# A two-layer hybrid trunk on one core: retention's gates computed as a block problem of seven products, with the mixer's work in another order

## The chip, the cores and the metric

The kernel runs on one core of one Trainium2 chip. The metric is the device time of one execution in microseconds (us). PE is the matrix engine, PEld its loading of the stationary operand, DVE the vector engine, ACT the scalar engine, POOL the GpSimd engine; SP issues most of the transfers, POOL the transfers that add to what already lies in the target ("accumulating").

## The reference, cut to what matters

Two layers; the input is one sequence of 512 rows of 1024 values, all float32. A layer's mixer projects the rows with one matrix of 9216 columns, runs three branches (retention, chunked attention, differential attention), weighs each with a gate, and projects the sum; a SwiGLU block follows.

```python
h = jnp.einsum('bsd,de->bse', x, w_in[l])
rq, rk, rv, rg, cq, ck, cv, dq, dk, dv, gates = jnp.split(h, splits, axis=-1)
o_a = _retention(rq, rk, rv, rg, ret_norm_g[l])      # rq and rk turned by a rotary table
o_b = _chunk_attention(cq, ck, cv, ca_rel_bias[l])
o_c = _diff_attention(dq, dk, dv, lam, lambda_init, da_norm_g[l])
g = jax.nn.sigmoid(gates + b_merge[l]).reshape(B, S, N_BRANCHES, D)
merged = (g[:, :, 0] * (o_a @ w_branch_a[l]) + g[:, :, 1] * (o_b @ w_branch_b[l])
          + g[:, :, 2] * (o_c @ w_branch_c[l]))
x = _layer_norm(DEEPNORM_ALPHA * x + merged @ w_out[l], ...)
ffn = (silu(u_gate) * u_up) @ w_ffn_out[l]           # u = x @ w_ffn_in[l]
x = _layer_norm(DEEPNORM_ALPHA * x + ffn, ...)
```

The change touches the 1024 columns of `gates` that belong to retention (`g[:, :, 0]`), one tile of the third branch's gates, and the order in which rq, rk, rv, rg, cv, dv and these gates are made.

## The kernel before, in words

**Numbers.** Each float32 operand is carried as a high part and the remainder. A product is therefore three matmuls (`mm3`, L126 to L128: high by high, low by high, high by low), all at the same shapes. A piece of a weight arrives by DMA in a staging tile `st` (four buffers of 1 MB), ACT copies its rounded high part to `wh` (L158 or L396), and DVE subtracts to get the low part `wl` (L159 or L403). `wh` and `wl` have three buffers each (`AHEAD`), so the copy of a block waits until PE has ended the block three places before it; a staging buffer is free again when DVE has read it for the last time.

**Block problems.** The large projections take two column groups and two halves of the 1024 inputs as a 2x2 block matrix and compute the result with seven products instead of eight. `u_two` (L911) lists the seven by name: m1, m2, y, v, x, g, h. A product's weight side is a staged block or a sum of blocks: the sum `a` is loaded by SP and a second block is added to it by an accumulating DMA from POOL (`more`, L192); the sum `d` is a loaded block to which DVE adds (L271); `c` is loaded and accumulated like `a`, and `e` is a further sum. Classes `Close`, `Early`, `Late` and `Known` differ in when blocks are loaded and added. The activation side is a quarter of x, or a left or right sum of quarters, which `s_q(k)` makes on DVE and ACT (L425 to L436, with the split of L110 and L116). A product is 24 matmuls of 512 columns and each of its lines is `pf<-...`; afterwards ACT copies the bank (`tc<-pf`, L928), or DVE adds it or subtracts it (L933, L938, L943). Where a text writes w, p and q, these are the problems of cv with dv and of the two halves of rv with rg.

**Gates.** The gates of a branch are made by `u_gate(br, i)`, 256 columns at a time: 48 matmuls of 512 columns with x as the stationary operand (`proj_T`, `pt<-xTh,wh`) and a tanh on ACT (L1283) whose tile goes to DRAM. Retention's four such items stand between the products of the mixer.

**Order.** `start` and the list behind it (L1467 to L1500) are the items of the mixer in the order in which PE runs them. The lists beside an item are functions that are called after its two halves. Weights are fetched `AHEAD` items early. A scheduler then emits one program for each engine, and each engine takes its own instructions strictly in that order. The indices COPIED_AT and ADDED_AT say at which item copies and sums for the later SwiGLU part are made.

**Opening.** In layer 0 PE first makes rq and rk tile by tile as weights land, with two weight tiles of 256 columns, then two gate tiles with a third (`u_first`, L913). Each rq or rk bank goes through the rotary table at once: `rotary` (L505) copies the swapped halves on ACT (L510) and multiplies and adds on DVE (L512 to L514).

## Time and profile before

| | us |
|---|---|
| median of 3 runs | 1844.89 (1843.74, 1844.89, 1845.23) |
| the profiled execution, its own time | 1843.16 |
| its span, first to last instruction | 1841.3 |
| PE busy in the span | 1830.8 |
| DVE busy | 1375.4 |
| ACT busy | 1035.2 |

The mean granted clock of PE was 0.999. A row of the timeline gives the start, the duration, the engine, the line and the tiles; a bracket at its end is the idle time before it with what ended it. A row of a group gives count, busy time and the mean of one in ns. PE's matmuls overlap, so what one costs is the distance from one start to the next, not its own duration.

### The profile page before, as it was taken

The page shows a single profiled execution, that of the slowest core. Times are in us where ns is not written, and L with a number is a line of the kernel's source. Part 1 is how long each engine was busy: PE and PEld are TensorE (multiplying, and loading weights), DVE is VectorE, ACT ScalarE, POOL GpSimd, SP SyncE. Part 2 cuts the span into 40 slices and gives each one's busy share as a digit, 9 for nine tenths or more (in the row PEclk, how much of TensorE's full clock was granted, in tenths as well). Part 3 has the DMA queues.
Part 4 walks back from the last instruction along what each step waited for, and adds up shares of the span by engine and source line. Part 5 has one row for each costly group of instructions (what it writes and reads, how often), then busy time and mean ns, then how long its engine had stood idle before and what let it go on. Part 6 is the DMA issues. An engine that isn't in the chain of part 4 may idle for free.

```text
span 1841.3 us, 23376 instructions
## 1 busy us (share of the span) xinstructions
PE 1830.8 (99%) x8718; PEld 1530.6 (83%) x8718; DVE 1375.4 (75%) x2077; ACT 1035.2 (56%) x1651; POOL 156.3 (8%) x170
## 2 busy tenths in 40 slices
PE   9999999999999999999999999999999999999998
PEld 8888888888887888888888888888888878888886
DVE  6866766767669786789787767566775797867887
ACT  5555555576545645555555556556766465455552
POOL 2001000001001000001020010000010010000010
PEclk9999999999999999999999999999999999999999
DMA  9689755566475876687685887555565677667783
GB/s 286 185 272 240 194 159 171 140 185 165 117 226 148 201 221 162 160 257 195 218 252 175 245 217 208 181 150 154 165 160 137 195 180 183 208 177 180 225 219 113
DMA packets 248065, 351.12 MB, mean 191 GB/s; under 512 B 9605, under 2 KB 112113, under 8 KB 247953
## 3 DMA queue, kind: packets, MB, share of 16 engines
q1 hardware_dynamic: 213088, 281.84, 46.2%
q0 software_dynamic: 34720, 67.55, 21.3%
q8 instruction: 68, 1.11, 0.2%
q14 instruction: 45, 0.36, 0.1%
q10 hardware_dynamic: 144, 0.26, 0.0%
HBM read 327.54 MB, written 64.01 MB: 213 GB/s over the span
## 4 chain that ended last, share of the span: by engine, by line
PE 97%; DVE 2%; ACT 1%; DMA 1%; issue 0%; POOL 0%; DVEq 0%; POOLq 0%; ACTq 0%
PE pf L126 16%; PE pf L128 15%; PE pf L127 15%; PE pt L126 14%; PE pt L128 13%; PE pt L127 13%; PE ptr L587 1%; PE psc L548 1%; PE pco L1159 1%; PE psc L547 1%; PE ph L1540 1%; PE pdo L1236 1%; DVE wl L403 1%; DMA st<-out10c 1%; ACT wh L396 0%; PE pro L128 0%
## 5 line engine op out<-in xcount | busy, mean ns | idle before, releaser
L403 DVE TENSOR_TENSOR wl<-st,wh 128x2048 fp32r<-128x2048 f32 (+2 forms) x173 | 377.9, 2185 | 153.3 <-ACT wh L396 152.8
L396 ACT CAST wh<-st 128x2048 fp32r<-128x2048 f32 (+1 forms) x168 | 315.2, 1878 | 237.9 <-PE pf L128 110.8
L126 PE MATMUL pt<-xTh,wh 128*128 128x512 f32 x832 | 326.8, 393 | 0.0
L128 PE MATMUL pt<-xTh,wl 128*128 128x512 f32 x832 | 324.4, 390 | 0.0
L127 PE MATMUL pt<-xTl,wh 128*128 128x512 f32 x832 | 324.2, 390 | 0.0
L159 DVE TENSOR_TENSOR wl<-st,wh 128x1024 fp32r<-128x1024 f32 (+2 forms) x158 | 166.6, 1073 | 60.8 <-ACT wh L158 47.5
L158 ACT CAST wh<-st 128x1024 fp32r<-128x1024 f32 (+2 forms) x158 | 143.6, 929 | 83.4 <-PE pt L127 58.1
L128 PEld LDWEIGHTS pt<-xTh,wl 128*128 128x128 f32 x832 | 156.2, 188 | 33.1
L127 PEld LDWEIGHTS pt<-xTl,wh 128*128 128x128 f32 x832 | 156.4, 188 | 31.2 <-DVE xTl L757 0.3
L126 PEld LDWEIGHTS pt<-xTh,wh 128*128 128x128 f32 x832 | 156.4, 188 | 31.0
L126 PE MATMUL pf<-wh,xTh 128*128 128x512 f32 x384 | 151.1, 395 | 0.2
L128 PE MATMUL pf<-wh,xTl 128*128 128x512 f32 x384 | 149.2, 390 | 0.0
L127 PE MATMUL pf<-wl,xTh 128*128 128x512 f32 x384 | 149.2, 389 | 0.0
L126 PE MATMUL pf<-wh,s12h 128*128 128x512 f32 x296 | 116.7, 394 | 0.0
L126 PE MATMUL pf<-wh,s43h 128*128 128x512 f32 x296 | 116.0, 392 | 0.0
L127 PE MATMUL pf<-wl,s12h 128*128 128x512 f32 x296 | 115.4, 390 | 0.0
L127 PE MATMUL pf<-wl,s43h 128*128 128x512 f32 x296 | 115.3, 389 | 0.0
L128 PE MATMUL pf<-wh,s43l 128*128 128x512 f32 x296 | 114.9, 389 | 0.0
L128 PE MATMUL pf<-wh,s12l 128*128 128x512 f32 x296 | 114.7, 390 | 0.0
L928 ACT COPY tc<-pf 128x512 f32<-128x512 f32 x96 | 55.2, 588 | 72.0 <-PE pf L128 71.0
L126 PEld LDWEIGHTS pf<-wh,xTh 128*128 128x128 f32 x384 | 72.1, 188 | 17.1 <-ACT xTh L110 1.5
L128 PEld LDWEIGHTS pf<-wh,xTl 128*128 128x128 f32 x384 | 72.1, 188 | 16.0 <-DVE xTl L116 0.7
(384 smaller groups left out, 3685.9 us busy)
## 6 DMA issues: line engine op xcount, KB each, us to landing
st<-in_w_in SPq DMA_DIRECT2D x53, 1024.0 KB, 6.7
st<-in_w_ffn_in SPq DMA_DIRECT2D x46, 1024.0 KB, 5.3
st<-in_w_in SPq DMA_DIRECT2D x48, 512.0 KB, 5.0
st<-in_w_ffn_in POOLq DMA_DIRECT2D x20, 1024.0 KB, 11.1
st<-in_w_in POOLq DMA_DIRECT2D x12, 1024.0 KB, 11.5
st<-in_w_ffn_out SPq DMA_DIRECT2D x12, 1024.0 KB, 5.2
th<-th SPq DMA_DIRECT2D x40, 256.0 KB, 4.8
st<-in_w_out SPq DMA_DIRECT2D x10, 1024.0 KB, 6.0
```

The lines of the kernel that those rows point to most:

```text
L126: nc.tensor.matmul(ps, lh, rh, start=start, stop=False, skip_group_check=onto)
L127: nc.tensor.matmul(ps, lh, rl, start=False, stop=False, skip_group_check=onto)
L128: nc.tensor.matmul(ps, ll, rh, start=False, stop=stop, skip_group_check=onto)
L158: return [nc.scalar.copy(self.hi[:, a:b], self.st[:, a:b]), nc.vector.tensor_sub(self.lo[:, a:b], self.st[:, a:b], f(self.hi[:, a:b]))]
L159: nc.vector.tensor_sub(self.lo[:, a:b], self.st[:, a:b], f(self.hi[:, a:b]))]
L396: nc.scalar.copy(self.hi, st)
L403: nc.vector.tensor_sub(self.lo[:, k], self.st[:, k], f(self.hi[:, k]))
L547: yield nc.tensor.matmul(ps[:, :w], self.q[j][:, n], self.k[j][:, :w], start=True, stop=False)
L548: yield nc.tensor.matmul(ps[:, :w], self.q[j][:, n], self.kl[j][:, :w], start=False, stop=True)
L587: nc.tensor.transpose(ps[:, o + P * (nt - mt):o + P * (nt - mt) + P], E[pk][:, c + P * mt:c + P * mt + P], ident)
L928: nc.scalar.copy(t[to, j], ps)
L1159: pin(nc.tensor.matmul(*ops[k], start=k == order[0], stop=k == order[-1]))
```

## The change

Retention's gates leave `u_gate` and become a fourth block problem, t, of class `Early`, over the 1024 gate columns. It uses `product_T` in place of `product`: a block of 128 by 128 of the weight is the stationary operand and a quarter of the rows, 256 columns wide, is the moving one, so a product is 48 matmuls of 256 columns. The tanh is taken on 256 columns at a time with the bias of a column tile, and a tile goes to DRAM as one half of a pair.

The order of the mixer's first part is written anew, with t's products between those of w and p, and q's behind p's. Counted over both layers, 384 `pt` matmuls of 512 columns leave (832 to 704 in each of the three lines of `mm3`), and 672 `pf` matmuls of 256 columns come in. DVE gets 17 instructions more (12 `tc` additions, 4 sums of staging tiles, and the sizes of some subtractions change), ACT 34 more, SP three transfers more and POOL four more accumulating transfers.

Three smaller things go with it: the first problem is of a new class `Grown`, whose first block grows into the sum `a`; in the opening the rq and rk banks are only copied (`raw`) and swapped on ACT, and `s_rot` does the DVE part later, behind products of t and w; values that went to DRAM come back in halves (`v_back`), and lam is computed later (`late_lam`).

```diff
-EARLY = [(0, 0), (0, 1), (0, 2), (0, 3), (2, 0)]
+EARLY = [(2, 0)]
...
+    class Grown(Early):
+        def m1(self):
+            if "made" in self.__dict__:
+                return self.__dict__.pop("made")
+            if "first" not in self.__dict__:
+                self.early()
+            self.a = self.__dict__.pop("first")
+            b = self.block(self.a)
+            self.more(self.a, 0, 1)
+            return b
...
+    def product_T(acts, name, j, wt, ps=None):
+        onto = ps is not None
+        ps = ps if onto else bank("pf")
+        for q in range(2):
+            c, o = P * (2 * j + q), 256 * q
+            for k in range(wt.nk):
+                hi, lo = acts[k].use[name]
+                mm3(ps[:, o:o + 256], wt.hi[:, k, c:c + P], wt.lo[:, k, c:c + P], hi, lo,
+                    k == q == 0 and not onto, q == 1 and k == wt.nk - 1, True)
+        return ps
...
+        def rqk_raw(i, h, ps):
+            t = g(name="raw")
+            nc.scalar.copy(t, ps)
+            raws[i, h] = t, swapped(ps, 64)
+
+        def s_rot(i, h):
+            return lambda: rqk_done((rq, rk)[i], h, *raws.pop((i, h)))
...
+                    vectors()
                     quarters(0)
+                    opening[0].made = opening[0].m1()
+                    for k in range(2):
+                        s_q(k)()
                 for i, w in enumerate(wts):
...
                         if i < 2:
-                            rqk_done((rq, rk)[i], j, ps)
+                            rqk_raw(i, j, ps)
                         else:
-                            gate_done(0, j, ps)
+                            gate_done(2, 4 * j, ps)
...
+        def gates_left(base):
+            def done(t, c):
+                i, j = divmod(t, 2)
+                m = base // 2 + j
...
+                s = g(name="th") if i and base == 0 else c
+                for q in range(2):
+                    sl = slice(256 * q, 256 * q + 256)
+                    d = 2 * m + q
+                    nc.scalar.activation(s[:, sl], c[:, sl], AF.Tanh, scale=0.5, bias=v["hb"][:, d:d + 1])
+                nc.sync.dma_start(th["pair", m][:, :, 256 * i:256 * i + 256], s.rearrange("p (q c) -> p q c", q=2))
+            return done
...
-        opening[l] = (Early if l else Close)(W, 0, 4, (CV, DV))
+        opening[l] = Grown(W, 0, 4, (CV, DV))
...
+        t = u_two(Early(W, 0, 4, (GATE, GATE + 512)), xq, gates_left(0), gates_left(4), product_T)
+        natural = []
         if l == 0:
-            start = [(u_first(),), (u_gate(0, 1), [s_q(0), s_q(1)], [s_q(2), w["a"]]), (u_gate(0, 2), [s_q(3)], [w["c"]]),
-                     (w["m1"],), (w["y"],), (w["v"],), (w["m2"], [lam])]
+            start = [(u_first(), [], [s_q(2)], [], [s_q(3)]),
+                     (w["m1"],), (w["m2"],)]
...
-            (w["x"], [p["a"]]), (u_gate(0, 3), [s_kt(0)], [s_kt(1)]), (w["g"],), (w["h"], [p["c"]]),
-            (p["m1"], [s_dh(0)]), (p["y"], [], [s_r1(0)]), (p["v"], [s_dh(1)]), (p["m2"], [], [s_r1(1)]),
-            (p["x"], [q["a"]]), (u_rqk(rq, RQ, 1), [s_kv(0)], [s_kv(1)]), (p["g"], [q["c"]]), (p["h"],),
...
+            (t["m1"], [w["c"]], natural[1:2]), (w["y"], natural[2:3]), (w["v"], [t["a"]]), (w["x"], natural[3:]), (t["m2"], [s_rot(1, 0)]),
+            (w["g"],), (t["y"], [s_kt(0)]), (w["h"], [t["c"]], [s_rot(1, 1)]), (t["v"], [p["a"]], [s_rot(0, 0)]),
+            (t["x"], [], [s_rot(0, 1)]), (p["m1"], [s_dh(0)], [s_kt(1)]), (t["g"], [late_lam]),
+            (p["y"], [], [s_r1(0)]), (t["h"], [p["c"], s_dh(1)]), (p["v"],), (p["m2"], [q["a"]], [s_r1(1)]), (p["x"],),
+            (q["m1"], [s_kv(0)], [s_kv(1)]), (p["g"],), (q["y"],), (p["h"], [q["c"]]),
```

The scheduled programs of the changed kernel show three places. The first is DVE in the opening of layer 0, where the low parts of the first blocks of w are made between quarter sums (`sa`, `sb` and their low parts `s12l`, `s43l`). Before, with the end of the third quarter's sums, the fourth quarter's, and among them the low part for w's v, the third of its blocks (`wl_634`):

```order
L435 TENSOR_TENSOR sb_542<-xf_134,sa_535 128x256
L436 TENSOR_TENSOR sb_542<-xf_122 128x256
L116 TENSOR_TENSOR s43l_546<-sb_542,s43h_545 128x512
L425 TENSOR_TENSOR sa_585<-xf_125,xf_137 128x256
L426 TENSOR_TENSOR sa_585<-sa_585,xf_125 128x256
L403 TENSOR_TENSOR wl_634<-st_631,wh_633 128x2048
L116 TENSOR_TENSOR s12l_589<-sa_585,s12h_588 128x512
L435 TENSOR_TENSOR sb_592<-xf_137,sa_585 128x256
L436 TENSOR_TENSOR sb_592<-xf_125 128x256
L271 TENSOR_TENSOR st_631<-st_631,st_549 128x2048
```

Now, with `wl_466` the low part for w's m2, in two halves:

```order
L116 TENSOR_TENSOR s43l_378<-sb_374,s43h_377 128x512
L542 TENSOR_TENSOR sw_383<-sw_383,sinr_198 128x512
L438 TENSOR_TENSOR sa_391<-xf_125,xf_137 128x256
L439 TENSOR_TENSOR sa_391<-sa_391,xf_125 128x256
L416 TENSOR_TENSOR wl_466<-st_463,wh_465 128x1024
L116 TENSOR_TENSOR s12l_395<-sa_391,s12h_394 128x512
L448 TENSOR_TENSOR sb_398<-xf_137,sa_391 128x256
L449 TENSOR_TENSOR sb_398<-xf_125 128x256
L416 TENSOR_TENSOR wl_466<-st_463,wh_465 128x1024
```

The last quarter sums stood around the third block of w; now they stand ahead of and between the halves of its second one, with the rotary's multiplications (`sw`) among them. On ACT the same place reads now as follows; `raw` and `sw` are the copies of the rq and rk banks, `wh_324` and `wh_465` the high parts for m1 and m2:

```order
L110 CAST s43h_353<-sb_350 128x512
L886 COPY raw_357<-pt_201 128x512
L409 CAST wh_324<-st_322 128x2048
L838 COPY colv_312<-pcol_310 128x64
L534 COPY sw_359<-pt_201 64x512 x2
L886 COPY raw_362<-pt_202 128x512
L534 COPY sw_364<-pt_202 64x512 x2
L409 CAST wh_465<-st_463 128x2048
L110 CAST s12h_370<-sa_367 128x512
L110 CAST s43h_377<-sb_374 128x512
L886 COPY raw_381<-pt_203 128x512
L534 COPY sw_383<-pt_203 64x512 x2
```

Behind the high part of m2 come two quarter sums' splits and the third bank's copies, on which the DVE rows above wait. The second place is DVE between t's y and t's x in layer 0 (`wl_748` and `wl_939`; `wl_820` is for w's h, `wl_872` for t's v):

```order
L416 TENSOR_TENSOR wl_748<-st_680,wh_747 128x2048
L116 TENSOR_TENSOR vhl_737<-tc12_695,vhl_737 128x2x128
L116 TENSOR_TENSOR vhl_742<-tc12_695,vhl_742 128x2x128
L980 TENSOR_TENSOR tc11_590<-tc11_590,pf_751 128x512
L541 TENSOR_TENSOR rot_781<-raw_381,cosr_197 128x512
L980 TENSOR_TENSOR tc11_620<-tc11_620,pf_789 128x512
L543 TENSOR_TENSOR rot_781<-rot_781,sw_383 128x512
L416 TENSOR_TENSOR wl_820<-st_626,wh_819 128x2048
L116 TENSOR_TENSOR rqkl_786<-rot_781,rqkh_785 128x512
```

These rows run on without a gap into the next ones:

```order
L990 TENSOR_TENSOR tc22_642<-tc22_642,pf_476 128x512
L990 TENSOR_TENSOR tc22_657<-tc22_657,pf_491 128x512
L416 TENSOR_TENSOR wl_872<-st_869,wh_871 128x2048
L116 TENSOR_TENSOR vhl_836<-tc22_642,vhl_836 128x2x128
L116 TENSOR_TENSOR vhl_841<-tc22_642,vhl_841 128x2x128
L116 TENSOR_TENSOR vhl_859<-tc22_657,vhl_859 128x2x128
L116 TENSOR_TENSOR vhl_864<-tc22_657,vhl_864 128x2x128
L271 TENSOR_TENSOR st_869<-st_869,st_680 128x2048
L118 SCALAR_TENSOR_TENSOR kT_906<-pkt_903,rcol_86,kT_906 128x128
L300 TENSOR_TENSOR st_942<-st_942,st_869 128x2048
L118 SCALAR_TENSOR_TENSOR kT_906<-pkt_903,rcol_86,kT_906 128x128
L416 TENSOR_TENSOR wl_939<-st_869,wh_938 128x2048
```

Rotary rows (`rot`) and w's evictions (`tc`, `vhl`) now lie between the low parts of t's blocks, where an item of `u_gate` puts only the low part of its weight on DVE. The third place is DVE again, from w's v to t's a, the buffer of which comes free behind it (`st_558` is w's d, `wl_623` the low part for w's x):

```order
L416 TENSOR_TENSOR wl_561<-st_558,wh_560 128x2048
L116 TENSOR_TENSOR vhl_548<-tc11_504,vhl_548 128x4x64
L116 TENSOR_TENSOR vhl_553<-tc11_504,vhl_553 128x4x64
L271 TENSOR_TENSOR st_558<-st_558,st_322 128x2048
L300 TENSOR_TENSOR st_626<-st_626,st_558 128x2048
L416 TENSOR_TENSOR wl_623<-st_558,wh_622 128x2048
```

On SP the load of t's a (`st_680`, whose buffer was `st_558`'s) is followed by others that wait in turn:

```order
L187 DMA st_659<-in_w_in 128x4x512
L187 DMA st_680<-in_w_in 128x4x512
L187 DMA st_869<-in_w_in 128x4x512
L187 DMA st_942<-in_w_in 128x4x512
L1125 DMA v0_128_0_0_717<-vhl_714 128x512
```

Before, the load of p's a (`st_834`) stood behind a gate weight and a tile of gates:

```order
L154 DMA st_737<-in_w_in 128x8x256
L1287 DMA th0_0_5_626<-th_624 128x512
L187 DMA st_834<-in_w_in 128x4x512
L187 DMA st_938<-in_w_in 128x4x512
L1078 DMA v0_64_0_0_762<-vhl_759 128x512
```

52 lines of the change are left out of this document (31 added, 21 removed).

## The prediction

> **What bounds the kernel now.** I read the page first, then the waits of PE, the stretches of time, the chain, and last the rows of the places that change.
>
> ```profile
> span 1841.3 us, 23376 instructions
> PE 1830.8 (99%) x8718; PEld 1530.6 (83%) x8718; DVE 1375.4 (75%) x2077; ACT 1035.2 (56%) x1651; POOL 156.3 (8%) x170
> PE 97%; DVE 2%; ACT 1%; DMA 1%; issue 0%; POOL 0%; DVEq 0%; POOLq 0%; ACTq 0%
> PE warm L732 <- POOL ident masks.py:199: 1.5, 1, 1.5
> PE pf L126 <- DVE z L1387: 0.5, 1, 0.5
> PE px L656 <- DVE z L638: 0.3, 1, 0.3
> SPq L187 <- DVE wl L403: 495.4, 85, 16.0
> 100.00:150.00 50.00, 50.00 (x237) 41.95 (x236) 37.40 (x43) 28.05 (x40) 3.61 (x3) 1.00 0.85 253
> ```
>
> PE is busy for 1830.8 of 1841.3 us, carries 97% of the chain, and its three longest waits together are 2.3 us. So matmul time taken out comes off the end, and any new wait of PE goes on it. The last row is a stretch inside the mixer (us, then the busy time of PE, PEld, DVE, ACT, POOL, the clock, DMA's share, GB/s): DVE has 37.4 of 50 us in use, not enough to bind on average. But SP's queue waits 495.4 us for DVE's subtractions: a load starts when DVE gives its buffer back. DVE thus times the transfers, and a stretch with more DVE work than PE work can make PE wait where nothing waits now.
>
> **Step 1, matmul time.** The chain of the stretch 170 to 200 us shows the distance from one start to the next.
>
> ```profile
> 174.28 0.11 PE pro L126
> 177.15 0.23 PE pf L126
> 179.90 0.23 PE pt L126
> 190.78 0.87 PE prt L1060 x8
> L126 PE MATMUL pro<-rvh,rph x32: 277/283/283, 168.5 to 1167.0; 128*128 128x256 f32 x32
> L126 PE MATMUL pt<-xTh,wh 128*128 128x512 f32 x832 | 326.8, 393 | 0.0
> ```
>
> Between 174.28 and 177.15 lie 24 matmuls of 256 columns: 2.87 us, 120 ns each. Between 179.90 and 190.78 lie the 48 of 512 columns of one `u_gate` item: 10.88 us, 227 ns each. A block of 512 columns costs 24 x 0.227 = 5.44 us, t's product of 48 half as wide 5.76 us. The change takes out 384 x 0.2267 = 87.05 us and puts in 672 x 0.120 = 80.6 us: **-6.4 us**, 3.2 in each layer. The sums of a seven-product form are DVE's and cost PE nothing by themselves.
>
> The Trainium skill, page "TensorE: Matmul & The Clock Gate", section "Back-to-back issue gap", speaks against this trade: in a stream of weight loads and matmuls it gives 81 ns for 128 columns and 131 ns for 512. An estimate in between, 98 ns for 256 columns, would make it 672 x 0.098 - 384 x 0.131 = +15.6 us. The trace disagrees, with 120 and 227 ns at a granted clock of 1.00. The same section's formula for a single matmul (N/2.4 + 2.5, so 109 and 216 ns) would save 9.7 us (384 x 0.216 - 672 x 0.109); it lies nearer, and the rows stand.
>
> **Step 2, the opening of layer 0.** These are rows of ACT, DVE and PE, the start and the duration of each.
>
> ```profile
> 39.05 1.18 ACT L510 COPY sw<-pt 64x512 f32<-64x512 f32 x2
> 40.25 1.91 ACT L396 CAST wh<-st 128x2048 fp32r<-128x2048 f32 x1
> 23.04 2.36 DVE L159 TENSOR_TENSOR wl<-st,wh 128x1024 fp32r<-128x1024 f32 x2 [2.73 <-ACT wh L158]
> 42.20 2.29 DVE L403 TENSOR_TENSOR wl<-st,wh 128x2048 fp32r<-128x2048 f32 x1
> 44.41 0.69 DVE L116 TENSOR_TENSOR rqkl<-rot,rqkh 128x512 fp32r<-128x512 f32 x1
> 45.01 0.69 DVE L512 TENSOR_TENSOR rot<-pt,cosr 128x512 f32<-128x512 f32 x1
> 54.58 0.42 DVE L425 TENSOR_TENSOR sa<-xf 128x256 f32<-128x256 f32 x1
> 56.15 0.69 DVE L116 TENSOR_TENSOR s12l<-sa,s12h 128x512 fp32r<-128x512 f32 x1 [0.69 <-ACT s12h L110]
> 58.81 0.42 DVE L425 TENSOR_TENSOR sa<-xf 128x256 f32<-128x256 f32 x1
> 27.49 0.50 PE L126 MATMUL pt<-xTh,wh 128*128 128x512 f32 x1
> L928 ACT COPY tc<-pf 128x512 f32<-128x512 f32 x96 | 55.2, 588 | 72.0 <-PE pf L128 71.0
> ```
>
> From start to start a block's subtraction occupies DVE for 2.21 us (42.20 to 44.41) and a 512-wide instruction for 0.60. One quarter's sums take 4.23 us (54.58 to 58.81), because DVE and ACT wait for each other in turn. PE begins the third weight at 27.49 and ends its 48 matmuls at 38.4; m1 of w is then due, and m2 at 38.4 + 5.4 = 43.9. Before, gate items of 10.9 us each stood here and covered the quarter sums; now nothing does.
>
> DVE ends the third weight's low part at about 25.8 (23.04 + 2.36 and two small rows). Two quarters bring it to 25.8 + 2 x 4.23 = 34.3. ACT copies a bank (a raw copy is not in this trace; the nearest is the `tc` copy at 0.59), then casts m1's block to 36.1, DVE subtracts to 38.4: m1 is just in time. ACT then has two swaps, a raw copy and a small one ahead of m2's cast, which ends at about 41.0, and after it two splits of the third quarter, which that quarter waits for, and the next raw copy and swap to about 45.4. DVE's low part of m2 stands behind the product of this swap and two rows of the fourth quarter: 45.4 + 0.6 + 0.8 + 1.2 = 48.1 for the first half; the second, behind three more rows, at 50.6. PE starts m2 4.2 late and loses about 1 more at the second half, as its first six matmuls cover 1.4 of 2.5 us. I take **+5.0 us**. Bounds: 0 if the swaps go through ACT earlier (5 us of ACT rows are what has to move), 6.2 if PE waits for the second half from the start (50.6 less 43.9, less little).
>
> **Step 3, the block sum that t's y needs.** Its four rows in the groups and the transfers of the mixer, and the same thing in the SwiGLU part, where such problems already run into each other:
>
> ```profile
> st<-in_w_in SPq DMA_DIRECT2D x13, 1024.0 KB, 6.6
> st<-in_w_in POOLq DMA_DIRECT2D x4, 1024.0 KB, 12.1
> st<-in_w_ffn_in SPq DMA_DIRECT2D x15, 1024.0 KB, 5.3
> st<-in_w_ffn_in POOLq DMA_DIRECT2D x5, 1024.0 KB, 11.3
> 745.07 2.29 DVE L403 TENSOR_TENSOR wl<-st,wh 128x2048 fp32r<-128x2048 f32 x1
> 753.95 0.48 PE L126 MATMUL pf<-wh,s12h 128*128 128x512 f32 x1
> 753.18 1.28 POOL L192 DMA_DIRECT2D st<-in_w_ffn_in  x1 [14.93 <-DVE wl L403]
> 766.12 1.91 ACT L396 CAST wh<-st 128x2048 fp32r<-128x2048 f32 x1 [8.95 <-DMA st<-in_w_ffn_in]
> 768.07 2.29 DVE L403 TENSOR_TENSOR wl<-st,wh 128x2048 fp32r<-128x2048 f32 x1 [6.79 <-ACT wh L396]
> 770.36 0.39 PE L126 MATMUL pf<-wh,s12h 128*128 128x512 f32 x1
> ```
>
> Read the last six, but for PE's row at 753.95, as one chain: a subtraction ends at 747.36 and frees a buffer, the load and the accumulating transfer fill it until 766.1, cast and subtraction end at 770.36, and PE takes the block in that very moment: 23.0 us, no slack. From the transfers' medians a chain costs 5.3 + 11.3 + 1.9 + 2.3 plus 0.5 to hand over = 21.3 us, with the mixer's 6.6 + 12.1 it is 23.4. I take 22.
>
> In the new order t's a takes the buffer of w's d, whose last reader is the low part for w's x. Laid end to end after m2 (50.6), DVE's rows up to there are four subtractions, two staging sums, four 512-wide rows and four of 0.34: 6 x 2.21 + 4 x 0.6 + 4 x 0.34 = 17.0, with the waits for m2's banks about 18.6, so 69.2. With m2 begun at 48.9 PE reaches w's x at 48.9 + 3 x 5.44 + 5.76 = 71.0, and t's y after 5.44 + 5.76 + 5.44 more, at 87.7. There are 87.7 - 69.2 = 18.5 us for 22: **3.5 late** in layer 0. In layer 1, without the opening's sums, x is ready 3.6 us ahead instead of 1.8, so 20.2 us: **1.8 late**. Bounds: 5 where transfers go at the mixer's 23.4, and 0 where DVE is ahead by as much as `wh`'s three buffers allow. That is 6.6 us for the block subtracted at 745.07, which PE took at 753.95; then 16.6 + 6.6 = 23.2 are there for 22.
>
> **Step 4, DVE between t's y and t's x.**
>
> ```profile
> L403 DVE TENSOR_TENSOR wl<-st,wh 128x2048 fp32r<-128x2048 f32 x19 | 43.5, 2291 | 25.8 <-ACT wh L396 25.7
> L271 DVE TENSOR_TENSOR st<-st 128x2048 f32<-128x2048 f32 x3 | 6.9, 2285 | 0.0
> L933 DVE TENSOR_TENSOR tc<-tc,pf 128x512 f32<-128x512 f32 x6 | 4.1, 679 | 0.0
> L116 DVE TENSOR_TENSOR vhl<-tc,vhl 128x256 fp32r<-128x256 f32 x12 | 4.5, 419 | 0.7 <-ACT vhl L110 0.7
> L118 DVE SCALAR_TENSOR_TENSOR kT<-pkt,rcol,kT 128x128 fp32r<-128x128 f32 x8 | 2.8, 346 | 1.2 <-ACT kT L112 1.2
> ```
>
> The changed program has there three subtractions and two staging sums (5 x 2.21), seven 512-wide rows (4.2), six `vhl` (6 x 0.34, the 419 ns less the overlap) and two `kT` (0.54): 17.8 us without a gap, 19 with the idle time that these rows show. I take 18.3. PE has t's y, w's h and t's v there, 2 x 5.76 + 5.44 and 0.2 of transposes = 17.1. DVE starts even, since it waited for the late a, so t's x is **1.2 late** in each layer (0 to 2).
>
> **Step 5, p's a** waits in the same way for the low part of t's x, which ends when PE starts it. Until p's y there are 5.76 + 5.44 + 5.76 + 0.2 = 17.2 us for 22: **4.8 late** per layer. Where t's x had the lead of 3 to 4 us of step 3 this is 0.5 to 1.5, with 6 us nothing. q's a has 24 us, c of each problem as much or more: nothing.
>
> **What else moves at nothing.** The 34 ACT and 17 DVE instructions lie under PE (DVE's share of the stretch above is 75%); DVE's are 11 subtractions of 2048 for 10 of 1024, four sums and 12 additions, 11 x 2.21 - 10 x 1.2 + 4 x 2.21 + 12 x 0.6 = 28 us, which is what it would cost with no cover, and steps 2 and 4 count what I see uncovered. Four accumulating transfers of 1 MB come in, at a DMA share of 0.85 there: this may stretch the chains of steps 3 and 5 and is in their bounds. The halves of `v_back`, lam and the indices for the later sums lie where blocks are ready long ahead. SP's loads of t's c and p's a stand behind t's a in one queue, and are later by the same amounts.
>
> **Sum.** -6.4 + 5.0 + (3.5 + 1.2 + 4.8) + (1.8 + 1.2 + 4.8) = +15.9 us. The profiled execution took 1843.2, 1.7 under the median: 1859.1 there, and **1860.8** as a median.
>
> **Rivals.** *DVE keeps ahead (faster).* The chain at 770.36 shows that such problems can run into each other with no stall, with 23.0 us to spend, and DVE has a quarter of its time idle. If the opening is also covered, only -6.4 remains: 1838.5. Against it: in the SwiGLU part no rotary rows and `vhl` splits stand between the sums. *Only the opening shows (no change).* The low part of m2 is late by 5.0 and everything behind recovers, as PE's wait is itself a lead for DVE: -6.4 + 5.0 gives 1843.5. *The trade itself fails (slower, in another way):* two matmuls of 256 columns need two loads of the stationary operand where one of 512 needs one. From 129.5 ns (87.05/672) on nothing is saved; at 131 ns step 1 would be +1.0 and the whole 1868. Against it are the `pro` rows, the same shape at 120 ns. The Trainium skill's sustained figures, in the section named above, are such a rule; the trace has its own pitches for both widths, so I give it little.
>
> **How the numbers follow.** Stalls as in the sum, in part or in full (anything over +3.7): 0.57, of which 0.02 the failed trade. Opening alone or small stalls that cancel: 0.15. No stall to speak of: 0.28. A measurement of this kernel tells 0.2%, 3.7 us, from no change; faster is under 1841.2 and slower over 1848.6. The likeliest case's own range is 1848 to 1867, from the bounds of steps 2 to 5 (the low end with the opening and half of layer 0's other waits, the high end with 23.4 us in place of 22 for each of four chains). The range has to reach the no-stall case for 8 in 10: 1837 to 1867.
>
> **What would show it.** Step 1: `pf` matmuls of 256 columns at 120 ns from start to start, and PE's busy time down by 6.4. Step 2: a wait of PE for `wl` of 1024 columns at about 44 to 50 us. Steps 3 and 5: waits of PE for `wl` in four places, with a cast just ahead that waited for a POOL transfer. Step 4: DVE without idle time between t's y and t's x. PE waiting for nothing but its 2.3 us makes steps 2 to 5 wrong at once, and a wait for a bank or for ACT would be something that I have not seen.

## The result: 2.9% slower, in three parts

| | before | changed |
|---|---|---|
| median, us | 1844.62 (1843.74 to 1845.23, 4 runs) | 1899.22 (1892.27 to 1901.73, 4 runs) |
| profiled execution, own time | 1843.16 | 1892.27 |
| its span | 1841.3 | 1890.5 |

The ratio is 1.029, 95% interval 1.0263 to 1.0318. The prediction said slower, 1860.8 with a range of 1837 to 1867, so the way was right and the size was not: +54.6 us, where +15.9 was forecast. The profiled execution is the fastest of the four; it is 49.1 us above that of the kernel before.

The page of the changed kernel, its first lines:

```profile
span 1890.5 us, 24058 instructions
PE 1843.9 (98%) x9006; PEld 1550.1 (82%) x9006; DVE 1401.4 (74%) x2094; ACT 1053.2 (56%) x1685; POOL 157.4 (8%) x174
```

PE's waits there (us in all, times, longest us):

```profile
PE pf L127 <- DVE wl L416: 11.7, 6, 3.4
PE pro L126 <- ACT tc L975: 8.0, 3, 4.1
PE pf L128 <- DVE wl L416: 4.8, 2, 3.4
PE pf L126 <- ACT wh L409: 4.6, 3, 2.0
PE pt L126 <- DVE ro L1094: 3.9, 4, 1.3
```

Where there were three waits of 2.3 us together there are now some 39 us, mostly for the low part (`wl`) or the high part (`wh`) of a block. And PE, which was to be busy 6.4 us less, is busy 13.1 us more (1843.9 against 1830.8). Five stretches of 4 us in layer 0 show why. The columns are as in the row of the stretch 100 to 150 us of the prediction; PEclk is the third from the end:

```profile
112.00:116.00 4.00, 2.51 (x21) 2.30 (x20) 0.00 (x0) 1.43 (x1) 0.00 (x0) 1.00 1.05 358
116.00:120.00 4.00, 1.66 (x5) 1.17 (x6) 3.50 (x5) 3.18 (x5) 1.27 (x1) 0.96 0.35 100
120.00:124.00 4.00, 4.00 (x13) 3.07 (x11) 4.00 (x6) 1.59 (x3) 0.00 (x0) 0.61 0.98 208
132.00:136.00 4.00, 0.60 (x2) 0.30 (x2) 3.93 (x6) 4.00 (x12) 0.00 (x0) 1.00 0.67 240
136.00:140.00 4.00, 4.00 (x12) 3.16 (x11) 3.28 (x5) 4.00 (x5) 0.00 (x0) 0.59 0.31 78
```

PE is busy for 1.66 of 4 us, waiting, and in the 4 us behind it the clock is 0.61: PE is fully busy there with 13 matmuls, where a stretch at full clock holds 17 or 18 of this width (4 us / 227 ns). The same again behind 132 to 136. The kernel before has a clock of 1.00 in each of these stretches. So a long wait is paid twice. A finer stretch shows the clock at half:

```profile
119.67:123.08 3.41, 3.41 (x10) 2.63 (x9) 3.41 (x4) 1.79 (x4) 0.00 (x0) 0.50 0.98 184
```

I take the two apart by the distance from one matmul's start to the next: what is over the usual distance of its shape by more than 0.3 us counts as a wait, what is over it by less as slow matmuls. Waits: 42.3 us against 1.4 before. Slow matmuls: 28.4 against 14.0. With step 1 that is -6.4 + 40.9 + 14.4 = 48.9 us, of 49.1 measured. By place, both layers together:

| place | predicted | waits | slow matmuls behind them |
|---|---|---|---|
| step 1, matmul time | -6.4 | -6.4 | |
| step 2, opening of layer 0 | 5.0 | 3.1 | 1.5 |
| step 3, t's y | 3.5 + 1.8 | 1.6 + 5.4 | 2.2 |
| step 4, t's x | 1.2 + 1.2 | 0 | 0 |
| step 5, p's y, with p's m1 ahead of it | 4.8 + 4.8 | 8.0 + 5.2 | 4.9 |
| first cq/ck items, behind q | 0 | 4.9 + 5.8 | 4.4 |
| all others | 0 | 6.9 | 1.4 |

PE's waits at w's m2 (the opening, 47.50) and at t's y in both layers:

```profile
47.50 0.50 PE L127 MATMUL pf<-wl,xTh 128*128 128x512 f32 x1 [2.57 <-DVE wl L416]
90.75 0.39 PE L128 MATMUL pf<-s12h,wl 128*128 128x256 f32 x1 [1.42 <-DVE wl L416]
1026.49 0.39 PE L126 MATMUL pf<-s12h,wh 128*128 128x256 f32 x1 [1.64 <-ACT wh L409]
1030.39 0.58 PE L128 MATMUL pf<-s12h,wl 128*128 128x256 f32 x1 [3.40 <-DVE wl L416]
```

Step 1 itself holds. One product of t, 48 matmuls of 256 columns, runs from the first row to the second in 5.81 us, 121 ns each:

```profile
144.00 0.33 PE L126 MATMUL pf<-xTh,wh 128*128 128x256 f32 x1
149.81 0.40 PE L126 MATMUL pf<-wh,s43h 128*128 128x512 f32 x1
```

The stall at p's m1 and y in layer 0, first the transfers of 60 to 140 us (count, size, median us to landing):

```profile
st<-in_w_in SPq DMA_DIRECT2D x9, 1024.0 KB, 10.9
st<-in_w_in POOLq DMA_DIRECT2D x3, 1024.0 KB, 12.0
```

Then the timelines of the engines (start, duration, engine, line, and in brackets the idle time before):

```profile
102.04 1.27 POOL L192 DMA_DIRECT2D st<-in_w_in  x1 [25.81 <-DMA st<-in_w_in]
103.54 5.76 SPq L187 DMA_DIRECT2D st<-in_w_in  x2
114.57 1.90 ACT L409 CAST wh<-st 128x2048 fp32r<-128x2048 f32 x1 [8.53 <-PE pf L128]
116.50 2.29 DVE L416 TENSOR_TENSOR wl<-st,wh 128x2048 fp32r<-128x2048 f32 x1 [7.73 <-ACT wh L409]
116.52 0.50 PE L126 MATMUL pf<-wh,xTh 128*128 128x512 f32 x1 [2.01 <-ACT wh L409]
118.85 0.50 PE L127 MATMUL pf<-wl,xTh 128*128 128x512 f32 x1 [1.82 <-DVE wl L416]
117.70 1.27 POOL L192 DMA_DIRECT2D st<-in_w_in  x1 [14.39 <-DMA st<-in_w_in]
129.83 1.91 ACT L409 CAST wh<-st 128x2048 fp32r<-128x2048 f32 x1 [7.21 <-DMA st<-in_w_in]
133.35 2.29 DVE L416 TENSOR_TENSOR wl<-st,wh 128x2048 fp32r<-128x2048 f32 x1
135.69 0.50 PE L127 MATMUL pf<-wl,s12h 128*128 128x512 f32 x1 [3.40 <-DVE wl L416]
```

A plain load of 1 MB has a median of 10.9 us here; in the same 80 us of the kernel before it was 6.4. SP's row is two issues, p's m1 at 103.5 and p's a at 108.9. The first shares the DMA engines with the accumulating transfer of t's c (issued at 102.0), lands at 114.5 after 10.9 us, and PE waits twice, for the high part at 116.5 and for the low part at 118.85. The second lands after 8.2 us and is followed by its own accumulating transfer (117.7, 12.0 us). The chain of p's a, from 108.9 to the end of the subtraction at 135.6, takes 26.7 us, not 22; of these, 1.6 us are rows of the rotary that DVE takes between the end of the cast and the subtraction.

The stall ahead of the first cq/ck item in layer 0:

```profile
190.68 0.37 SPq L154 DMA_DIRECT2D st<-in_w_in  x1
190.78 1.29 POOL L356 DMA_DIRECT2D in0a<-in_w_ffn_in  x1 [0.98 <-DMA in0a<-in_w_ffn_in]
206.27 1.99 ACT L158 CAST wh<-st 128x1024 fp32r<-128x1024 f32 x2 [14.70 <-DMA st<-in_w_in]
208.17 0.58 ACT L975 COPY tc<-pf 128x512 f32<-128x512 f32 x1
208.80 0.58 PE L126 MATMUL pro<-rvh,rph 128*128 128x256 f32 x1 [4.07 <-ACT tc L975]
```

The weight of that item and an accumulating transfer for the SwiGLU part (`in0a`) are issued within 0.1 us; the weight lands after 15.5 us. (An accumulating transfer of q, issued at 188.5, is in flight as well.) ACT's cast of it stands in the queue ahead of the copy of a finished bank, so ACT idles 14.7 us, and PE, which wants that bank, waits 4.07 us for a copy of 0.58.

### The profile page after: what moved, and what is told of

Same layout as the page of the kernel before. It is cut to its first block, busy times and chain, and to the rows that moved or that the text cites. A ratio compares the mean times of both kernels' runs of the same rounds, so it can differ in the third digit from the quotient of the medians.

```text
span 1890.5 us, 24058 instructions
## 1 busy us (share of the span) xinstructions
PE 1843.9 (98%) x9006; PEld 1550.1 (82%) x9006; DVE 1401.4 (74%) x2094; ACT 1053.2 (56%) x1685; POOL 157.4 (8%) x174
## 5 line engine op out<-in xcount | busy, mean ns | idle before, releaser
L416 DVE TENSOR_TENSOR wl<-st,wh 128x2048 fp32r<-128x2048 f32 (+2 forms) x190 | 409.9, 2158 | 168.3 <-ACT wh L409 168.0
L409 ACT CAST wh<-st 128x2048 fp32r<-128x2048 f32 (+1 forms) x182 | 341.8, 1879 | 289.6 <-PE pf L128 106.3
L126 PE MATMUL pt<-xTh,wh 128*128 128x512 f32 x704 | 278.0, 396 | 3.9 <-DVE ro L1094 3.9
L128 PE MATMUL pt<-xTh,wl 128*128 128x512 f32 x704 | 274.6, 390 | 0.0
L127 PE MATMUL pt<-xTl,wh 128*128 128x512 f32 x704 | 274.5, 390 | 0.0
L159 DVE TENSOR_TENSOR wl<-st,wh 128x1024 fp32r<-128x1024 f32 (+2 forms) x142 | 147.5, 1055 | 63.3 <-ACT wh L158 54.4
L126 PEld LDWEIGHTS pt<-xTh,wh 128*128 128x128 f32 x704 | 132.8, 189 | 30.6 <-DVE ro L1094 4.7
L128 PEld LDWEIGHTS pt<-xTh,wl 128*128 128x128 f32 x704 | 132.3, 188 | 28.3
L127 PEld LDWEIGHTS pt<-xTl,wh 128*128 128x128 f32 x704 | 132.5, 188 | 26.1
L127 PEld LDWEIGHTS pf<-wl,xTh 128*128 128x128 f32 x384 | 73.2, 191 | 22.0 <-DVE wl L416 7.9
## 6 DMA issues: line engine op xcount, KB each, us to landing
st<-in_w_ffn_in POOLq DMA_DIRECT2D x20, 1024.0 KB, 11.4
```

What stands on the lines that cost most here:

```text
L126: nc.tensor.matmul(ps, lh, rh, start=start, stop=False, skip_group_check=onto)
L127: nc.tensor.matmul(ps, lh, rl, start=False, stop=False, skip_group_check=onto)
L128: nc.tensor.matmul(ps, ll, rh, start=False, stop=stop, skip_group_check=onto)
L159: nc.vector.tensor_sub(self.lo[:, a:b], self.st[:, a:b], f(self.hi[:, a:b]))]
L409: nc.scalar.copy(self.hi, st)
L416: nc.vector.tensor_sub(self.lo[:, k], self.st[:, k], f(self.hi[:, k]))
```

## The experiments

**One accumulating transfer less (t's c).**

```diff
-            self.more(self.c, 1, 1)
+            self.cols[0] == GATE or self.more(self.c, 1, 1)
```

> The changed kernel, but the accumulating transfer that completes t's block sum c is left out in both layers (so the gates of retention are not the reference's). In the changed kernel p's m1 waits in layer 0 (2.2 + 2.1 us at 116 to 119) and layer 1 (1.1 + 2.1 us at 1056 to 1058) for a plain load of 1 MB that took 10.9 us instead of 5 to 6, while that accumulating transfer was in flight. Theory 'shared transfers': the load takes about 6 us, both waits go, and with them the slow matmuls behind them; the whole is 8 to 11 us shorter. Rival 'buffers': what is late is the start of the load, which waits for DVE to free a staging buffer; the waits stay within 1 us and the time moves by less than 3 us.

1900.73 us: nothing gained. The wait at p's m1 is gone in both layers, and its load took 5.4 us in layer 0, so the shared transfer was a cause of that wait. But p's y, the next product but one, now waits longer:

```profile
135.46 0.80 PE L126 MATMUL pf<-wh,s12h 128*128 128x512 f32 x1 [5.41 <-ACT wh L409]
139.36 0.80 PE L127 MATMUL pf<-wl,s12h 128*128 128x512 f32 x1 [3.11 <-DVE wl L416]
```

That is 5.4 + 3.1 us in place of 2.0 + 1.8 at m1 and 3.4 at y; in layer 1, 3.4 + 3.1 us stand at y. PE came at p's y only 1.7 us earlier in layer 0 than in the changed kernel's profile, and no earlier in layer 1. The block itself came 3.7 and 6.2 us later: the accumulating transfer of p's a took 15.9 and 14.9 us, where it had taken 12.0 and 10.2. The waits at t's y were longer too, 2.2 + 1.8 us in layer 0 where 1.4 stood, though the program is the same up to there; the accumulating transfer of t's a had taken 14.0 us in place of 11.4. So the theory's time, 8 to 11 us less, was wrong, and one run does not tell whether these longer transfers come from the edit or vary by themselves.

**One accumulating transfer less (t's a).**

```diff
-            self.more(self.a, 0, 1)
+            self.cols[0] == GATE or self.more(self.a, 0, 1)
```

> The changed kernel, but the accumulating transfer that completes t's block sum a is left out in both layers (so the gates of retention are not the reference's). Theory of step 3 (the chain load, accumulate, cast, subtract is longer than the three products it has): the waits at t's y, 1.6 us in layer 0 and 1.8 + 3.6 us in layer 1, go, with some 2 us of slow matmuls behind the one of layer 1: 8 to 9 us shorter. Rival: PE is late there for DVE's order (rows of rotary and evictions ahead of the low part); then at least 1 us stays at each place.

1881.93 us, 10 us under the fastest run of the changed kernel and 17 under its median. The waits at t's y are gone in both layers, and so is that at p's m1; p's y waits 4.1 + 3.7 us in layer 0 and 4.8 + 3.7 in layer 1. Step 3's mechanism is shown: without its accumulating transfer, t's y waits for nothing.

**No accumulating transfers for the sums a of t and p.**

```diff
-            self.more(self.a, 0, 1)
+            self.cols[0] in (GATE, RV) or self.more(self.a, 0, 1)
```

> The changed kernel, but the accumulating transfers that complete the block sums a of t, p and q are left out in both layers (the gates of retention and its values and gate rg are not the reference's). Leaving out t's alone moved the wait to p's y (4.1 + 3.7 us in layer 0, 4.8 + 3.7 in layer 1). Theory 'chains of accumulated sums': with p's gone too nothing over 1.5 us is left between the opening and the first cq/ck item; with no_add_a at 1881.9 and these waits and their slow matmuls (about 19 us) away: 1860 to 1866. Rival 'DVE's order': p's y or a neighbour still waits for over 2 us in each layer, and the time stays over 1870.

The expectation says t, p and q, but the edit does something else. It asks for the first column of a block problem: q's is RV + 512, so q's a is still accumulated, and one problem of the SwiGLU part begins at column 1024, which is RV's value, so its sum is left out in both layers (its accumulating transfers fall from 20 to 18, those of the mixer from 16 to 12). PE waits for nothing in the SwiGLU part of either profile, but for one wait near the end.

1865.24 us, inside 1860 to 1866. Two groups of waits fill what is left, the opening's and those at the first cq/ck and branch items, and between them only one of 0.6 us stays:

```profile
PE pro L126 <- ACT tc L975: 8.3, 2, 5.1
PE pt L126 <- DVE ro L1094: 5.1, 4, 1.5
PE pf L127 <- DVE wl L416: 3.4, 1, 3.4
```

So the chains of these sums of t and p, with the slow matmuls behind them, are some 27 to 34 us of the 55. DVE's order of rows was not late by itself: with all of DVE's work still there, none of its rows holds PE for more than 0.6 us between the opening and the first cq/ck item. q's sum a, still made, cost PE nothing.

This run also shows what p's m1 needs to stall. Its load was issued at 97.2 here and again took 10.9 us beside the transfer of t's c, but PE came to p's m1 only at 112.05, 14.8 us after the issue, and did not wait. In the changed kernel PE came 10.8 us after it (103.5 to 114.35). So the slow load stalls PE there because DVE, held up by the late t's a, gave the buffer back with less time to spare; without the late t's a here, or without the transfer beside it in the run without t's c's, the wait goes.

**The copies for the SwiGLU part behind q's products.**

```diff
-COPIED_AT = [23, 26, 28, 31, 40, 43, 46, 48, 50, 52]
-ADDED_AT = [26, 28, 31, 33, 43, 46, 48, 50, 52, 54]
+COPIED_AT = [31, 33, 35, 37, 40, 43, 46, 48, 50, 52]
+ADDED_AT = [33, 35, 37, 39, 43, 46, 48, 50, 52, 54]
```

> The changed kernel with the eight copies and sums for the SwiGLU part that begin at items 23 to 33 moved to items 31 to 39, behind the last products of q. Theory 'shared transfers': the weight of the first cq/ck item lands about 6 to 8 us after its issue instead of 15.5, ACT's queue is not held by its cast for 14.7 us, and the waits of PE for the copy of a bank (4.1 us at 209, 3.9 + 0.5 at 1147, with 0.7 and 1.4 behind) go together with the slow matmuls behind them: 12 to 15 us shorter. Rival 'order on ACT': the cast stands ahead of that copy in ACT's order and its buffer is late anyway: at least 2 us stay at each of the two places.

1888.47 us. The waits for the copy of a bank (`pro` behind `tc`) are gone in both layers, so their cause was the copies and sums that ran beside the weight's load; 1.7 us for `ro` stays in layer 0. The time moved by 4 us against the fastest run and by 11 against the median, less than the 12 to 15 expected, and p's y in layer 1 waited 2.9 + 3.7 us here in place of 1.6.

**The rotary's swap later.**

```diff
-            raws[i, h] = t, swapped(ps, 64)
+            raws[i, h] = t
...
-            return lambda: rqk_done((rq, rk)[i], h, *raws.pop((i, h)))
+            return lambda: rqk_done((rq, rk)[i], h, raws.pop((i, h)))
```

> The changed kernel, but the swapped halves of the four rq and rk banks are made from the raw copy when the rotary is finished, not in the opening: four times two ACT copies (4.7 us) and four DVE products leave the opening of layer 0. Theory of step 2 (ACT and DVE rows ahead of the low part of w's m2): its wait of 2.7 + 0.4 us at 47 to 50 shrinks to under 1 us, and with it 1.5 us of slow matmuls: 3 to 5 us shorter. Rival: the quarter sums alone hold the low part: the wait stays over 2 us.

1905.66 us. The opening's wait went from 3.1 us to 1.5 (0.6 + 0.9) without slow matmuls behind it, so ACT's and DVE's rows there were part of the cause, as step 2 has it. PE then waited 3.0 us for a bank's copy at 66, where 0.7 us stood, 2.0 + 1.8 us at t's y of layer 0 in place of 1.4, and 9.8 us at 139 for the subtraction behind an x. That subtraction stands on DVE behind the low part of p's a, whose cast had waited 9.35 us for its transfer: the late p's a again, now met one product further on. That the moved rows made it later is not shown; the time did not fall.

**Matmuls in the gaps.**

```diff
+    def fill(ps, n, xs):
+        for i in range(n):
+            nc.tensor.matmul(ps, xs[i % 4].hi[:, :P], xs[4 + i % 4].hi, start=True, stop=True)
...
```

> The changed kernel, with matmuls that compute nothing needed (one high part of x against another, 512 columns, into the bank that the product overwrites) ahead of three products: 6 and 14 at t's y (layers 0 and 1), 13 at p's m1, 14 at p's y, 74 in all or 16.8 us of PE work, each put where PE waits anyway (1.6 and 5.4 us; 4.3 and 3.2; 3.7 and 1.6). Theory 'clock': the slow matmuls behind a wait of 2 us or more (pitch over 227 ns, 14 us more of them in the changed kernel than before, some 6.7 us at these places) come from the clock that is granted after idle time; filled waits leave the clock at 1.00 there, and in spite of 16.8 us more work the time falls by 2 to 8 us below the changed kernel's. Rival 'slow for another reason' (operands that arrive late, memory): the slow matmuls stay and the time rises by 3 to 8 us, the part of the fill that is longer than its wait.

1897.57 us, with 16.8 us more of PE work no slower than the changed kernel's median. In layer 0 the wait at p's m1 shrank to 1.3 us and none over 0.5 us is left at p's y, and the clock is 1.00 there where it was 0.61 and 0.59:

```profile
118.00:122.00 4.00, 4.00 (x21) 3.12 (x20) 1.17 (x1) 2.45 (x3) 0.01 (x1) 1.00 0.86 334
122.00:126.00 4.00, 2.86 (x13) 2.36 (x13) 3.32 (x6) 2.18 (x3) 1.27 (x1) 1.00 0.51 73
138.00:142.00 4.00, 4.00 (x20) 3.30 (x19) 3.08 (x7) 1.86 (x6) 0.00 (x0) 1.00 0.66 201
```

Locally the theory holds. The gain of 2 to 8 us was not seen: waits elsewhere were longer in this run (3.8 us in the opening, 1.2 + 1.8 us at t's y of layer 0, 5.7 at the cq/ck item), and why is not shown.

**t undone, the order kept.**

```diff
-            (t["m1"], [w["c"]], natural[1:2]), (w["y"], natural[2:3]), (w["v"], [t["a"]]), (w["x"], natural[3:]), (t["m2"], [s_rot(1, 0)]),
-            (w["g"],), (t["y"], [s_kt(0)]), (w["h"], [t["c"]], [s_rot(1, 1)]), (t["v"], [p["a"]], [s_rot(0, 0)]),
+            (u_gate(0, 0), [w["c"]], natural[1:2]), (w["y"], natural[2:3]), (w["v"],), (w["x"], natural[3:]), (u_gate(0, 1), [s_rot(1, 0)]),
+            (w["g"], [s_kt(0)]), (w["h"], [], [s_rot(1, 1)]), (u_gate(0, 2), [p["a"]], [s_rot(0, 0), s_rot(0, 1)]),
...
```

> The changed kernel with t undone: retention's gates are again four items of 48 matmuls of 512 columns, standing at four of the places of t's products, and everything else (the order of w, p and q, Grown, the rotary later, values back in halves) as changed; the indices of the copies for the SwiGLU part are shifted by the three items that are fewer. Theory of steps 3 to 5 (t's sums and the products too short to cover them): the waits at t's y, p's m1 and p's y go to under 1 us each; the opening (3.1 us and 1.5 of slow matmuls) and the waits ahead of the first cq/ck items (10 us with slow matmuls in each layer) stay; without the 6.4 us of step 1 this is 1858 to 1870. Rival 'the order alone': p's y still waits for over 3 us, and the time stays over 1875.

1859.36 us, inside 1858 to 1870. Nothing waits for t's or p's blocks; the waits that remain are the opening's and those around the first cq/ck items:

```profile
PE pt L126 <- DVE ro L1094: 6.0, 4, 1.9
PE pf L127 <- DVE wl L416: 4.1, 2, 3.3
PE pro L126 <- ACT tc L975: 1.9, 3, 1.0
```

So t as a block problem, with its functions at their places in the order, costs some 33 to 40 us of the 55, net of the 6.4 that it saves, and the rest of the change about 13 to 15. The opening's wait of 3.3 us had no slow matmuls behind it here.

**Two causes taken away together.** The edit of the copies on top of the kernel without sums a, and on top of the one with t undone (there the indices are three lower).

> The changed kernel without the accumulating transfers of the sums a of t, p and q (those gates and values are not the reference's), and with the copies for the SwiGLU part behind q's products: two of the causes found so far taken away together. If they add up, what is left is the opening (3 us and 1.5 to 2 of slow matmuls) and the 1.3 to 1.7 us waits of the branch items, less the 6.4 us of step 1: 1865.2 less the 12 us at the first cq/ck item of both layers, 1850 to 1855. If a stretch that is too full as a whole decides, the waits go elsewhere and it stays over 1858.

> The changed kernel with t undone (retention's gates as four items of 512 columns) and the copies for the SwiGLU part behind q's products. If the 15 us that this order lost against the kernel before were the opening and the copies, the waits at the first cq/ck item (2.8 us in layer 0, 3.7 and 1.7 of slow matmuls in layer 1) go and the opening's 4.4 and the 1.3 us waits remain: 1850 to 1854. Rival: it stays within 2 us of 1859.

1859.16 and 1857.00 us. In both the waits at the first cq/ck items are gone and the opening's is left, 4.0 us with 2.1 and 1.2 us of slow matmuls behind it. But the gains are 6 and 2 us where 10 to 15 and 5 to 9 were expected: waits of 0.5 to 1.8 us come up at the attention (`pco`, behind the moved copies) and at `ro`. Neither simple sum was right, though the named waits went; the rivals, over 1858 and within 2 us of 1859, describe the times better. (The first of the two kernels keeps q's a and leaves out the SwiGLU sum, as said above.)

**Other products between.** Two gate items of the second branch, 10.9 us each, moved into the mixer's first part, and the copies later.

```diff
...
+            (t["x"], [], [s_rot(0, 1)]), (u_gate(1, 2), [s_kt(1)]), (p["m1"], [s_dh(0)]), (t["g"], [late_lam]),
...
-            (u_gate(1, 1), [], d(2)[1]), (u_branch(1, 1), [s_d2(0)], d(3)[1]), (u_dqk(2), [s_d3(0)]),
-            (u_gate(1, 2), *d(4)), (u_branch(1, 2), *d(5)), (u_dqk(3), [v_back(dv, 1)]),
+            (u_branch(1, 1), d(2)[1], [s_d2(0)] + d(3)[1]), (u_dqk(2), [s_d3(0), gates_in(1, 2)]),
+            (u_dqk(3), [v_back(dv, 1)] + d(4)[0], d(4)[1]), (u_branch(1, 2), *d(5)),
```

> The changed kernel with its block problem t kept, but two gate items of the second branch (48 matmuls of 512 columns, no sums, no evictions on DVE) taken from later in the mixer and put where time is short: one behind the opening of layer 0 (in layer 1 between t's m2 and w's g) and one between t's x and p's m1; the copies for the SwiGLU part are moved behind q's last products. Theory: what was short is PE time between a release of a buffer and the product that needs it, 17 us where 22 to 27 are taken; with 10.9 us more in it the waits at p's m1 and p's y (8.0 and 4.8 us) go, and those of the opening and of layer 1's t's y with them; 1.6 at t's y of layer 0 and the 1.3 us ones stay. 1843 to 1856. Rival 'DVE and transfers have too much to do over the whole stretch': the waits move to q's products and to the attention that lost its cover, and the time stays over 1865.

1896.45 us. Layer 1's mixer has no wait over 0.6 us left until the first cq/ck item, t's y and p's y included: 10.9 us more between a release and the product that needs it are enough there. In layer 0 they were not: p's m1 still waits 0.8 + 1.8 us at 139.6 to 141.9. And the attention that lost these items now waits, and the new items themselves wait for their weights in layer 0:

```profile
PE psc L576 <- DVE ocl L118: 10.0, 2, 5.0
PE psc L576 <- ACT ks L110: 5.7, 2, 2.9
PE pt L126 <- ACT wh L158: 5.1, 2, 4.0
```

The rival was right in the time and in the attention's waits: each gate item had been the cover of something else.

**A try at a faster version.** Layer 0 as before; in layer 1 t with the second rk and rq items as the products between.

> An attempt at a version faster than both: layer 0 is the kernel before; layer 1 has t, with the second rk item between t's m2 and w's g and the second rq item between t's x and p's m1 in place of their later positions, the gate tile of the third branch and the first two cq/ck items where they stood before, and the copies for the SwiGLU part behind q's products. Theory (t is worth its 3.2 us per layer where 10.9 us of other products lie between a release and the product that needs it): no wait over 1 us in layer 1's mixer, 1841 to 1843. Rival (the stretch as a whole has too little slack, waits move on): waits of 2 us or more at q's products or the first cq/ck items, 1846 to 1856.

1865.31 us (median of 4), ratio 1.0107 (1.0086 to 1.0128) to the kernel before: 1.1% slower, above both the 1841 to 1843 of the theory and the 1846 to 1856 of its rival. The waits moved on, to t's m1 (2.5 us at 970), an m1 at 1043, a y at 1110 to 1114 (1.1 + 3.4) and the attention:

```profile
PE pf L127 <- DVE wl L416: 5.1, 2, 3.3
PE pf L126 <- ACT wh L409: 3.4, 2, 2.4
PE prt L1095 <- DVE ro L1082: 2.6, 2, 2.1
PE pco L1194 <- ACT cPh L110: 2.4, 1, 2.4
```

No version that beats the kernel before was found.

**The clock by itself.** The kernel before, with some subtractions repeated; no transfer is added.

```diff
+AGAIN = {40: 3, 49: 4, 58: 5, 67: 6, 120: 3, 129: 4, 138: 5, 147: 6}
...
-            for a in range(0, self.nk, step):
+            for a in [*range(0, self.nk, step)] + [0] * AGAIN.get(len(made), 0):
```

> The kernel before, with the subtraction that makes the low part of a block repeated 3, 4, 5 and 6 times more at four blocks of each layer's SwiGLU part (36 repeats of 2.2 us on DVE, the result unchanged), so that PE waits there by about 0, 1.5 to 2, 4 and 6 us, with nothing added to DMA or ACT. Theory 'clock': behind waits of about 2 us and more come matmuls slower than 227 ns for some us, with a granted clock near 0.5 to 0.6, 1 to 2.5 us of loss per wait; behind shorter waits none. Total 22 to 32 us of waits and 6 to 14 us of slow matmuls on top. Rival 'transfers' (the slow matmuls of the changed kernel come from its fuller DMA stretches or from operands that land late): under 2 us of slow matmuls in all.

1908.09 us. The longest wait, from PE's timeline:

```profile
851.66 0.79 PE L129 MATMUL pf<-wl,qm2h 128*128 128x512 f32 x1 [10.03 <-DVE wl L406]
```

The stretches in it and behind it:

```profile
846.00:851.50 5.50, 0.00 (x0) 0.00 (x0) 5.50 (x3) 0.00 (x0) 0.00 (x0) 0.54 0.11 14
851.50:856.00 4.50, 4.34 (x10) 3.46 (x11) 4.50 (x6) 1.66 (x3) 0.00 (x0) 0.50 1.01 390
856.00:861.00 5.00, 5.00 (x22) 4.05 (x21) 5.00 (x9) 1.72 (x1) 0.00 (x0) 0.94 0.75 263
```

The clock is 0.50 for the next 4.5 us, and 0.94 in the 5 us after that. In all there are 14.2 us of slow matmuls more than before, at the upper end of the 6 to 14 expected; the waits came to some 50 us, more than the 22 to 32 expected, as DVE was late for the next evictions too. The rival, which allowed under 2 us, falls.

## Why the prediction was wrong

**Step 1 was right.** 121 ns for 256 columns against 120 predicted, and the saving of 6.4 us is in the sum above. The rival of the failed trade falls. The sustained figures that the prediction quoted from the Trainium skill (page "TensorE: Matmul & The Clock Gate", section "Back-to-back issue gap", 131 ns for 512 columns) do not hold for these matmuls, which stand 227 ns apart.

**Step 2 had the place right and the wait too long.** The wait is where it was said, at the low part of w's m2, but 3.1 us for 5.0. That the whole loss there, 4.6 us with 1.5 of slow matmuls, is close to 5.0 is luck: the step had no term for slow matmuls.

**Step 3 had the right mechanism and place.** In layer 0 the chain took 22.0 us, from the load's issue at 68.7 to the end of the subtraction at 90.7, as estimated to the tenth; it began 0.5 us sooner and PE came 1.2 us later than reckoned, so 1.6 us of wait for 3.5. In layer 1 the term was too small: the accumulating transfer alone took 13.9 us, and PE waited 5.4 us for 1.8.

**Step 4 failed.** t's x was ready 0.4 us ahead in layer 0 and 2.0 in layer 1, not 1.2 late. DVE's rows were not the bound of this stretch; the run without the sums a of t and p shows the same.

**Step 5 had the right chain, and it was too short.** p's a took 26.7 us in layer 0 for an estimate of 22 and an upper bound of 23.4. That bound had 6.6 us for the load, which took 8.2, and nothing for the 1.6 us that DVE spent on the rotary's rows just ahead of the subtraction; the accumulating transfer took its 12.0. At p's y itself PE waited 3.7 and 1.6 us for the 4.8 and 4.8 predicted, less, as it had already lost 4.3 and 3.6 us at p's m1.

**"What else moves at nothing" is the step that failed most.** p's m1, a plain load, has no term in it. The prediction let a late t's a delay t's x and the accumulated sums behind it; but through DVE it delays more: DVE gives back the buffer of p's m1, and the load then took 10.9 us beside the accumulating transfer of t's c: 4.3 and 3.6 us of wait in the two layers. The prediction also set the later copies at nothing because blocks are ready long ahead there. They met the weight of the first cq/ck item, and ACT's order carried that to a bank that PE wanted: 10.7 us of waits in both layers together. A wait for a bank and for ACT is what the prediction had named as something that it had not seen.

**The sum left out a term.** It priced a wait at its length. Behind the long waits, and behind two of about 2 us close together, come slow matmuls, 14.4 us in all, and no term of the prediction had them. The one number in the profile of before that could have warned was that PE had no wait over 1.5 us anywhere: nothing there could show what a longer one does.

Of the range, 1867 as the high end was made from bounds that each held for its own term, with nothing for terms that I had not listed; those unlisted (p's m1, the cq/ck items, the clock, the small ones) are 8 + 11 + 14 + 7 = 40 us of waits and slow matmuls.

What stays open: why the four runs of the changed kernel spread over 9 us where those before spread over 1.5 (the accumulating transfer of t's a, 11.4 us in one profile and 14.0 in another with the same program up to there, is one place where runs differ), and which of the small waits (0.3 to 1.5 us, 6.9 us in all) belong to which part of the change. The waits for `ro` of 1.3 us came with every version of the new order that kept the first branch items where the change has them; they were not tried alone.

## What to carry to other kernels

Count a matmul engine that never waits as a balance, not as slack in the others: every item that covered a chain of load, accumulate, cast and subtract has to be replaced when it is taken out. Here t as a block problem saved 6.4 us of matmuls and cost 33 to 40 us more than that. Price a transfer by what flies beside it (here 5 to 6 us alone, 11 to 12 beside an accumulating one), and follow each engine's queue behind a cast that waits for such a transfer. A chain that is late also delays the engine that ends it, and so every buffer that this engine gives back behind it, even for plain loads. And judge an edit by the end of the stretch: a wait that went came back at the next chain.

## What the runs showed of the hardware

**A wait of PE of more than about 2.5 us is followed by half clock.** Over all the runs above I took the waits of 0.45 us or more with no other within 6 us. Of some 90 waits up to 2.46 us none was followed by more than about 0.5 us of slow matmuls; of 23 from 2.6 to 10.2 us, 22 were followed by about 1 to 2.7 us, whatever their length, and one of 3.18 us by 0.1. Waits close together count as well: 2.0 and 1.8 us at p's m1 brought half clock, while 3.3 us with 0.8 behind it, in the opening of the run with t undone, did not. The half clock needs no added transfers (the run with repeated subtractions) and it can be kept away by matmuls that compute nothing (the run with filled gaps). The Trainium skill, page "TensorE: Matmul & The Clock Gate", section "What's actually happening", has this: half clock after an idle window of about 3.4 us, full clock after as long a busy one, and a window that runs freely, so that the moment varies. The traces agree with the half (0.50 granted) and with the length: the stretches at half clock last 3.4 us (119.67 to 123.08 in the changed kernel), 6.8 (208.42 to 215.25) or 10.2 (846.39 to 856.63 in the run with repeated subtractions), one, two or three such windows, and part of a stretch can fall into the wait itself. They show the drop from 2.6 us of waiting on, earlier than that window, and the exceptions fit one that runs freely.

**An accumulating transfer can double the loads beside it.** The median load of 1 MB by SP in 60 to 140 us of layer 0 was 10.9 us in the changed kernel and 6.5 in the one without the sums a of t and p; the accumulating ones stayed at 12.0 and 12.4. Single loads show the same: 5.5 us at 96.0 with none beside it, 10.9 at 103.5 and 11.5 at 118.8, each issued 1.1 to 1.5 us behind an accumulating one. Not every load is slowed: one issued at 1083.5, 0.3 us ahead of an accumulating transfer, landed after 5.9 us. Other plain loads were in flight too, and their share is not told apart.
